# Reciprocal roots by Newton steps on VectorE, attention values with features on the partitions, low parts of weights on VectorE, and new tables of pulls

## The chip, the cores and the metric

The kernel runs on one core of a Trainium2 chip. A core has a matrix engine (TensorE, PE in the profile, its weight loads PEld), a vector engine (VectorE, DVE), a scalar engine (ScalarE, ACT), a general engine (GpSimd, POOL) and DMA queues (SP among others). Each engine works through its own queue in order, and semaphores hold an instruction until its inputs are there. The metric is the device time of one execution, in microseconds (us); before it is 652.63 us, the median of 3 runs (649.9 to 655.0).

## The reference

One layer of a streaming encoder over 512 tokens with 1024 features, cut to what is computed:

```
h = RMSNorm(x) * (1 + scale) + shift            # scale, shift, gate = adaLN(c)
p = h @ w_in                                    # one projection, split among the branches
y_a = RWKV7(p_a) * silu(g_a) @ w_a_out          # 8 heads of 64, decayed state, group norm
y_b = DSA(p_b) * silu(g_b) @ w_b_out            # 8 heads of 64, q and k RMS-normalised per head
m = sigmoid(p_ga) * y_a + sigmoid(p_gb) * y_b
x + gate * (m @ w_o)
```

The recurrence of RWKV7 is linear and is solved in chunks of 64 tokens. DSA scores the keys of each query with 8 small index heads, keeps the best (at most 128 here, within the chunks that are allowed), and takes a softmax over those:

```
idx_score = sum_h relu(iq_h @ ik) * iw_h;  sel = top_k(idx_score, 128)
p = softmax(q @ k_sel * 64**-0.5);  y = p @ v_sel
```

Everything is float32. The square roots are those of the RMS norm of x, of the norms of q and k, and of the group norm of the RWKV branch.

## The kernel before

**Precision.** A float32 operand of a large product is split in a high part that TensorE multiplies fast (type fp32r) and a low part, the rest. A projection is three products: high by high, low by high, high by low. Weights come by DMA from SP's queue (`wraw`), ScalarE copies the high part (`whi`, `whigh`), and a subtraction makes the low part (`wlo`, `wlow`, L247). Which engine subtracts is set by the block's place in the list of filler blocks: block 0 on VectorE, blocks 1 to 13 on GpSimd as soon as the high part is asked for, the later ones on VectorE two steps of the filler later (list `later`).

**Stages.** (1) Front, 0 to 64 us: x, its norm, adaLN, the transposes. (2) Index scores with the rates of decay, 64 to 135. (3) Preparation, 135 to 237: products, bonus and Gram matrices of the RWKV heads. (4) Solve, 237 to 311: triangular systems, column by column, on VectorE: a product (`pt`, L704) and a sum (`XT`, L706) for the even and the odd blocks. (5) Chain, 311 to 362: eight chunks in turn with a state `SV`. (6) Attention, 362 to 549: 32 jobs (4 pairs of heads, 4 blocks of 128 queries, 2 heads). (7) Merge and output, 549 to 648.

**What sets the order.** After the front the order is that of the code. A generator `main()` writes stages 2 to 6 piece by piece and yields after each piece two numbers: so many us of filler to draw into TensorE's queue (`pull`) and so many of side work to draw into VectorE's (`pull_dve`: top-k, group norm). The filler is the 24 projection blocks that the branches need later (`projections()`), about 10 us each; the side work of a finished block (copies on ScalarE, shifts on VectorE, roots) follows it through `later`. The tables `GT` and `DT` at the end of the function give the two numbers of the first 129 pieces; behind them, in the attention, defaults hold (1.3 us after each of two pieces of a job).

**A job of the attention.** `scores` makes two products into `ps_a`; one VectorE operation (L889) adds the mask and takes the minimum; ScalarE takes the exponential with its sum (`lg`, `sm`). One job later `flip` turns `lg` 128 columns at a time on TensorE, and ScalarE copies the result to `pT`. For each two jobs `values` multiplies `pT` (stationary, 128x128) by 64 columns of `vt`, so that tokens lie on the partitions; VectorE takes the reciprocal of the two sums (L913) and multiplies (L915, `yt`); `turn` transposes `yt` on TensorE into `ps_z`, and after four blocks one multiplication by the gate (L927) writes 128x512 of `yb`.

**Roots.** `qk_stats` (4 calls) and the group norm (2 calls) each take a square root on ScalarE, then a reciprocal on VectorE; `qk_stats` follows with one Newton step, and GpSimd scales `qn` by it (L833). ScalarE loads a table of functions (ACT_TABLE_LOAD) when it goes from an exponential to a root and back.

Of the kernel before, what the change touches and what calls it, by code (L numbers as in the profile page):

```python
# [37 lines left out]
def hybrid_block_kernel(ctx, tc, x, c, norm_w, w_ada, b_ada, w_in, mu, w0, w_up, a0, a_up, k_k, k_a,  # L38
# [67 lines left out]
    eps6 = cp.tile([128, 1], F32, name="eps6")  # L106
    V.memset(eps6, EPS)
    epsg = cp.tile([128, 1], F32, name="epsg")
    V.memset(epsg, GN_EPS)
# [18 lines left out]
    ss = cp.tile([128, NT], F32, name="ss")  # L128
    for i in range(NT):
        junk = T("LX6", [128, D], bufs=2, name="junk")  # L130
        act(junk, xt(i), AF.Square, accum_out=ss[:, i:i + 1])
    act(ss, ss, AF.Sqrt, scale=1.0 / D, bias=eps6)
    V.reciprocal(ss, ss)
    for i in range(NT):
        act(xt(i), xt(i), AF.Copy, scale=ss[:, i:i + 1])

# [735 lines left out]
    def attention():  # L872
# [45 lines left out]
        def turn():  # L918

            p, i, yt = st.pop("y")  # L920
            if i == 0:
                st["z"] = bank("z")
            tr(st["z"][:, i * 128:(i + 1) * 128], yt.rearrange("p s d -> p (s d)"), ident)
            if i == NT - 1:
                if p % 2 == 0:
                    ybt.append(T("kr", [128, 2, S], bufs=2, name="yb"))
                V.tensor_mul(ybt[p // 2][:, p % 2, :], st.pop("z"), sgb[p])  # L927
# [468 lines left out]
```

## Time and profile before

The profiled execution took 649.95 us, of which the span from its first to its last instruction is 648.2 us; the rest lies around it.

| stage, us | length | PE busy | DVE busy | ACT busy | POOL busy | granted clock |
|---|---|---|---|---|---|---|
| front 0-64 | 64 | 46.97 | 40.82 | 35.93 | 11.76 | 1.00 |
| index 64-135 | 71 | 59.66 | 47.37 | 44.27 | 15.26 | 0.92 |
| preparation 135-237 | 102 | 100.93 | 73.81 | 41.64 | 52.34 | 0.99 |
| solve 237-311 | 74 | 60.60 | 65.48 | 27.39 | 31.52 | 0.93 |
| chain 311-362 | 51 | 45.86 | 30.88 | 22.17 | 6.37 | 0.93 |
| attention 362-549 | 187 | 164.86 | 95.57 | 97.01 | 4.83 | 0.93 |
| merge, output 549-648 | 99 | 95.06 | 62.87 | 21.39 | 0.00 | 1.00 |

Busy us are read against the length of the stage: the engine with the largest share is the candidate for what bounds it, and the waits of the others say on whom they wait. The granted clock is that of TensorE, as a share of its full speed. An idle time in brackets names the instruction that ended it. Busy of TensorE counts a matmul until its modelled end.

### The profile page before, as it was taken

What the parts mean: (1) busy time and instruction counts of PE and PEld (TensorE: products, weight loads), DVE (VectorE), ACT (ScalarE), POOL (GpSimd) and SP (SyncE); (2) the same over time, 40 slices, a digit from 0 to 9 for tenths busy, and PEclk for the clock granted to TensorE, in tenths of its full rate; (3) what the DMA queues carried; (4) which work ended last, traced back from release to release, by engine and by line L of the source; (5) the groups of instructions that cost most, each with busy time, mean ns of one, the idle gap of its engine ahead of it and who ended that gap; (6) DMA issues with size and microseconds to landing.
All of it is one profiled execution on the core that took longest, in us unless ns stands there. A gap on an engine that the chain in (4) does not pass through costs nothing.

```text
span 648.2 us, 10436 instructions
## 1 busy us (share of the span) xinstructions
PE 573.9 (89%) x4051; PEld 475.2 (73%) x4051; DVE 416.8 (64%) x904; ACT 289.8 (45%) x521; POOL 122.1 (19%) x138
## 2 busy tenths in 40 slices
PE   1899888899999986997898799977987999999997
PEld 0677546567677966896776678876766888998997
DVE  4794537898769559996576664654554344888542
ACT  7743755652353333327433455555644445322210
POOL 7000202235264582352211000101000000000000
PEclk9999979989999997998799899968987999999999
DMA  9990312226546732145564121120212222656331
GB/s 300 320 332 10 98 32 66 66 47 166 139 122 167 170 101 73 46 130 147 179 231 148 29 70 52 48 65 19 75 39 65 66 66 81 179 176 205 115 122 66
DMA packets 80637, 75.00 MB, mean 116 GB/s; under 512 B 15737, under 2 KB 76226, under 8 KB 80588
## 3 DMA queue, kind: packets, MB, share of 16 engines
q1 hardware_dynamic: 74492, 59.86, 31.3%
q0 software_dynamic: 3776, 12.22, 6.2%
q10 hardware_dynamic: 2320, 2.26, 1.1%
q8 instruction: 32, 0.52, 0.3%
q14 instruction: 17, 0.14, 0.1%
HBM read 62.63 MB, written 11.55 MB: 114 GB/s over the span
## 4 chain that ended last, share of the span: by engine, by line
PE 58%; DVE 22%; ACT 13%; issue 3%; DMA 2%; POOL 1%; SPq 0%; POOLq 0%; ACTq 0%; DVEq 0%
PE ps_pj L46 32%; PE ps_yc L46 9%; PE ps_a L46 6%; DVE pt L704 5%; PE ps_o L46 3%; PE ps_z L46 3%; DVE XT L706 2%; ACT whi L87 2%; PE ps_a L49 2%; PE ps_yc L49 2%; DVE bias L90 2%; DVE wlo L247 2%; ACT qd L87 1%; DVE qd L90 1%; ACT L87 1%
## 5 line engine op out<-in xcount | busy, mean ns | idle before, releaser
L46 PE MATMUL ps_pj<-hh,whi 128*128 128x512 f32 (+1 forms) x304 | 126.5, 418 | 2.4 <-ACT hh L87 2.4
L46 PE MATMUL ps_pj<-hh,wlo 128*128 128x512 f32 (+1 forms) x304 | 127.2, 418 | 1.1 <-POOL wlo L247 1.1
L46 PE MATMUL ps_pj<-hl,whi 128*128 128x512 f32 (+1 forms) x304 | 126.3, 416 | 0.2 <-DVE hl L191 0.2
L247 POOL TENSOR_TENSOR wlo<-wraw,whi 128x1024 fp32r<-128x1024 f32 (+1 forms) x38 | 64.9, 1725 | 138.0 <-ACT whi L87 121.1
L87 ACT ACTIVATE whi<-wraw 128x1024 fp32r<-128x1024 f32 (+2 forms) x80 | 71.2, 918 | 26.7 <-DVE xr L1224 19.2
L46 PEld LDWEIGHTS ps_pj<-hh,whi 128*128 128x128 f32 (+1 forms) x304 | 59.5, 196 | 16.1 <-ACT hh L87 3.1
L46 PEld LDWEIGHTS ps_pj<-hh,wlo 128*128 128x128 f32 (+1 forms) x304 | 59.3, 195 | 16.3 <-issue 3.0
L46 PE MATMUL ps_pj<-whi,hh 128*128 128x256 f32 x192 | 58.8, 306 | 12.2 <-DVE sga L90 6.3
L46 PEld LDWEIGHTS ps_pj<-hl,whi 128*128 128x128 f32 (+1 forms) x304 | 59.5, 196 | 13.2 <-DVE hl L191 1.2
L247 DVE TENSOR_TENSOR wlo<-wraw,whi 128x1024 fp32r<-128x1024 f32 (+1 forms) x42 | 50.4, 1210 | 27.2 <-ACT whi L87 27.1
L46 PE MATMUL ps_pj<-wlo,hh 128*128 128x256 f32 x192 | 57.0, 297 | 0.4 <-POOL wlo L247 0.4
L46 PE MATMUL ps_pj<-whi,hl 128*128 128x256 f32 x192 | 56.9, 296 | 0.0
L46 PEld LDWEIGHTS ps_pj<-whi,hh 128*128 128x128 f32 x192 | 39.2, 204 | 14.1 <-DVE sga L90 7.0
L46 PEld LDWEIGHTS ps_pj<-wlo,hh 128*128 128x128 f32 x192 | 39.4, 205 | 0.7 <-POOL wlo L247 0.6
L46 PEld LDWEIGHTS ps_pj<-whi,hl 128*128 128x128 f32 x192 | 39.2, 204 | 0.0
L46 PE MATMUL ps_pj<-whi,mh 128*128 128x256 f32 x128 | 36.4, 285 | 0.0
L46 PE MATMUL ps_pj<-wlo,mh 128*128 128x256 f32 x128 | 36.0, 281 | 0.0
L46 PE MATMUL ps_pj<-whi,ml 128*128 128x256 f32 x128 | 36.0, 281 | 0.0
L87 ACT ACTIVATE lg<-lg,mx 128x128 f32<-128x128 f32 (+3 forms) x32 | 18.0, 562 | 38.7 <-DVE mx L889 27.2
L704 DVE TENSOR_TENSOR pt<-XT,PNO 128x2 f32<-128x2 f32 (+45 forms) x61 | 31.6, 557 | 0.1
L833 POOL TENSOR_TENSOR qn<-qn,s 128x256 f32<-128x256 f32 x16 | 11.1, 720 | 101.5 <-DVE s L90 79.1
L90 DVE SCALAR_TENSOR_TENSOR qd<-ps_a,P,qd 64x256 fp32r<-64x256 f32 x32 | 15.5, 483 | 20.1 <-ACT qd L87 20.1
(286 smaller groups left out, 1205.3 us busy)
## 6 DMA issues: line engine op xcount, KB each, us to landing
wraw<-in_w_in_dram SPq DMA_DIRECT2D x44, 512.0 KB
wa<-in_w_ada_dram SPq DMA_DIRECT2D x32, 256.0 KB
lxc<-dLX POOLq DMA_DIRECT2D x8, 768.0 KB, 5.3
wraw<-in_w_in_dram SPq DMA_DIRECT2D x18, 256.0 KB
dLX<-lx SPq DMA_DIRECT2D x8, 512.0 KB
wraw<-in_w_ada_dram SPq DMA_DIRECT2D x8, 512.0 KB
wraw<-in_w_o_dram SPq DMA_DIRECT2D x8, 512.0 KB
x<-in_x_dram SPq DMA_DIRECT2D x4, 512.0 KB
```

The costliest lines, as they stand in the source:

```text
L46: return nc.tensor.matmul(*a, **k)
L49: return nc.tensor.transpose(*a, **k)
L87: A.activation(o, i, func, **kw)
L90: V.scalar_tensor_tensor(o, a, s, b, op0=op0, op1=op1, **kw)
L247: eng.tensor_sub(l_, r_, f(h_))
L704: V.tensor_mul(pv[e], XT[e][:, a0:, j + 1:], PN[:, j, None, j + 1:].to_broadcast([128, m, n]))
L706: V.tensor_reduce(XT[e][:, (j + 2 - e) // 2:, j], pv[e], axis=AX.X, op=ALU.add)
L833: G.tensor_mul(qv, qv, bc(y[:, i, :]))
```

## The change

- A function `rsqrt` makes a reciprocal root of small tiles with 12 VectorE operations: an addition, a shift of the bits, a start value from integers, and three Newton steps of three operations. It takes the place of the square root on ScalarE and of the reciprocal in the norm of x (now in two pairs of token blocks), in `qk_stats` and in the group norm.
- `norm` divides the exponentials in place before they are turned: a reciprocal of a 128x1 tile and a multiplication of `lg` (128 to 512 columns) for each of the 32 jobs.
- `values` has 64 features of `vt` as the stationary tile and 128 columns of `pT` moving; the two heads of a job pair write the two halves of the partitions of one bank, banks `o` and `z` by turns. One multiplication by the gate (128x128) for each two jobs writes `yb`. `turn`, `yt` and the four large multiplications by the gate go.
- Low parts: all on VectorE, all through `later`. 22 subtractions of 128x1024 and 16 of 128x256 change their engine.
- The tables of pulls now cover all pieces (0 to 201). Added up, the drawn filler runs behind that of before by 2.5 us from piece 1 on, by 3 us or so through preparation and solve, is 1.8 us ahead from piece 105 (the end of the solve), 6.8 us ahead by piece 128 (the end of the chain), and 7 to 9.7 us ahead in the attention. The sum of the filler is the same.

```
+    def rsqrt(y, t_, u, eps, c):
+        V.tensor_scalar(u, u, eps, None, op0=ALU.add)
+        V.tensor_scalar(t_.bitcast(I32), u.bitcast(I32), 1, None, op0=ALU.logical_shift_right)
+        V.tensor_scalar(y.bitcast(I32), t_.bitcast(I32), -1.0, 1597463007.0, op0=ALU.mult, op1=ALU.add)
+        for k in (1.0, 1.0, c):
+            stt(t_, y, -0.5 * k, y, ALU.mult, ALU.mult)
+            V.tensor_mul(t_, t_, u)
+            stt(y, t_, 1.5 * k, y, ALU.add, ALU.mult)
...
             def low():
-                wlow(G if i < NPOOL else V, raw, hi, lo, 256, blocks[i][1])
+                wlow(V, raw, hi, lo, 256, blocks[i][1])
                 w_load()
-            if i < NPOOL:
-                low()
-            else:
-                later.append([2, low])
+            later.append([2, low])
...
     def qk_stats(g, j, s2, qn):
-        act(y, s2, AF.Sqrt, scale=1.0 / HD, bias=eps6)
-        V.reciprocal(y, y)
-        V.tensor_scalar(s2, s2, -0.5 / HD, -0.5 * EPS, op0=ALU.mult, op1=ALU.add)
-        V.tensor_mul(t_, y, y)
-        V.tensor_mul(t_, t_, s2)
-        stt(y, t_, 1.5, y, ALU.add, ALU.mult)
-        if j == 0:
-            V.tensor_scalar(y, y, -0.125, None, op0=ALU.mult)
+        rsqrt(y, t_, s2, EPS * HD, HD ** 0.5 if j else -1.0)
...
+        def norm(n):
+            p, i, s = jobs[n]
+            lg, sm = st[n], sums[p, i][:, s:s + 1]
+            V.reciprocal(sm, sm)
+            V.tensor_scalar(lg[:, :128 * (i + 1)], lg[:, :128 * (i + 1)], sm, None, op0=ALU.mult)
+
         def values(n):
-            ps = bank("o")
-            for s in range(2):
-                pT = st.pop(n + s)
-                for j in range(i + 1):
-                    mm(ps[:, 64 * s:64 * s + 64], pT[:, j * 128:(j + 1) * 128],
-                       vts[j // 2][:, j % 2, (2 * p + s) * 64:(2 * p + s + 1) * 64], start=(j == 0), stop=(j == i))
-            sm = sums.pop((p, i))
-            V.reciprocal(sm, sm)
-            yt = T("on", [128, 2, 64], bufs=2, name="yt")
-            V.tensor_mul(yt, ps[:, 0:128].rearrange("p (s d) -> p s d", d=64), bc(sm))
-            st["y"] = p, i, yt
+            pTs = [st.pop(n + s) for s in range(2)]
+            ps = bank("oz"[n // 2 % 2])
+            for j in range(i + 1):
+                for s in range(2):
+                    mm(ps[half(s), :128], vts[j // 2][:, j % 2, (2 * p + s) * 64:(2 * p + s + 1) * 64],
+                       pTs[s][:, j * 128:(j + 1) * 128], start=(j == 0), stop=(j == i))
+            ts_ = slice(i * 128, (i + 1) * 128)
+            V.tensor_mul(ybt[p // 2][:, p % 2, ts_], ps[:, :128], sgb[p][:, ts_])
...
+                if n:
+                    norm(n - 1)
                 scores(n)
                 yield gp(f"at1.{p}.{i}.{n % 2}")
             if n % 2 and n >= 3:
                 values(n - 3)
-            if n % 2 == 0 and n >= 4:
-                turn()
...
-        104: 2.404, 105: 2.512, 106: 2.635, 107: 0.78, 108: 2.528,
+        104: 2.404, 105: 5.754, 106: 2.635, 107: 0.78, 108: 2.748,
-        126: 1.751, 127: 4.016, 128: 0.054}
+        126: 1.969, 127: 6.028, 128: 0.347, 129: 0.82, 130: 1.08,
```

VectorE's queue in the solve before, from the sums behind the 105-column products on; `pt` and `XT` are the products and sums of the columns, and MATCH_REPLACE is a piece of the top-k.

```order
L706 TENSOR_REDUCE XT<-pt 128x7
L706 TENSOR_REDUCE XT<-pt 128x8
L516 MATCH_REPLACE bias_586<-m_2163,bias_586 128x512
L704 TENSOR_TENSOR pt<-XT,PNO 128x128 x2
L706 TENSOR_REDUCE XT<-pt 128x8 x2
L704 TENSOR_TENSOR pt<-XT,PNO 128x136
L704 TENSOR_TENSOR pt<-XT,PNO 128x153
L706 TENSOR_REDUCE XT<-pt 128x8
L706 TENSOR_REDUCE XT<-pt 128x9
```

The same place in the changed kernel; `wlo` is the low part of a weight, L1118 a sum of squares for the norm of q or k.

```order
L709 TENSOR_REDUCE XT<-pt 128x7
L709 TENSOR_REDUCE XT<-pt 128x8
L254 TENSOR_TENSOR wlo<-wraw,whi 128x1024
L519 MATCH_REPLACE bias_605<-m_2202,bias_605 128x512
L707 TENSOR_TENSOR pt<-XT,PNO 128x128 x2
L709 TENSOR_REDUCE XT<-pt 128x8 x2
L1118 TENSOR_REDUCE s_2178<-sq 128x4
L707 TENSOR_TENSOR pt<-XT,PNO 128x136
L707 TENSOR_TENSOR pt<-XT,PNO 128x153
L709 TENSOR_REDUCE XT<-pt 128x8
L709 TENSOR_REDUCE XT<-pt 128x9
L254 TENSOR_TENSOR wlo<-wraw,whi 128x1024
```

Two subtractions of 128x1024 now stand among the columns, where there was none; before, GpSimd's queue held them.

VectorE's queue in the attention before, from the first 512-key job to the first job of the next pair of heads; `lg,mx` is the mask step of a job, `ya` a piece of the other branch's output.

```order
L889 ISA lg,mx<-ps_a,bias_586 128x512
L889 ISA mx 128x1
L90 SCALAR_TENSOR_TENSOR ya<-ps_a,P_559,sga 128x256
L1031 TENSOR_TENSOR ya__3765<-ya,ya__3764 128x256
L90 SCALAR_TENSOR_TENSOR ya<-ps_a,P_559,sga 128x256
L1031 TENSOR_TENSOR ya__3765<-ya,ya__3764 128x256
L889 ISA lg,mx<-ps_a,bias_586 128x512
L889 ISA mx 128x1
L913 RECIPROCAL sm<-sm 128x2
L915 TENSOR_TENSOR yt<-ps_o,sm 128x128
L889 ISA lg,mx<-ps_a,bias_583 128x128
L889 ISA mx 128x1
```

The same jobs in the changed kernel, from the division of the first 512-key job on.

```order
L902 RECIPROCAL sm<-sm 128x1
L903 TENSOR_SCALAR lg<-lg,sm 128x512
L885 ISA lg,mx<-ps_a,bias_605 128x512
L885 ISA mx 128x1
L91 SCALAR_TENSOR_TENSOR ya<-ps_a,P_578,sga 128x256
L1020 TENSOR_TENSOR ya__3835<-ya,ya__3834 128x256
L91 SCALAR_TENSOR_TENSOR ya<-ps_a,P_578,sga 128x256
L1020 TENSOR_TENSOR ya__3835<-ya,ya__3834 128x256
L917 TENSOR_TENSOR yb<-ps_o,sgb 128x128
L902 RECIPROCAL sm<-sm 128x1
L903 TENSOR_SCALAR lg<-lg,sm 128x512
L885 ISA lg,mx<-ps_a,bias_602 128x128
```

The division of job n-1 (L902, L903) now stands ahead of the mask step of job n, and behind the pieces of `ya`, so that it is the exponential's sum for which VectorE may wait there; the step that writes `yb` reads TensorE's result with the gate, where `yt` was multiplied by the reciprocal.

TensorE's queue before, at the first values of a 512-key block; `ps_pj` is filler.

```order
L46 MATMUL ps_pj<-whi,hh 128x256
L46 MATMUL ps_pj<-wlo,hh 128x256
L46 MATMUL ps_pj<-whi,hl 128x256
L46 MATMUL ps_o<-vt,pT 128x64 x8
L49 MATMUL ps_yc<-ident,lg 128x128
```

And in the changed kernel.

```order
L47 MATMUL ps_pj<-whi,hh 128x256
L47 MATMUL ps_pj<-wlo,hh 128x256
L47 MATMUL ps_pj<-whi,hl 128x256
L47 MATMUL ps_z<-pT,vt 64x128 x8
L50 MATMUL ps_yc<-ident,lg 128x128
```

The eight products of the place stay eight; moving and stationary operand have changed sides, the output has 64 partitions and 128 columns, and the row for `ps_z<-ident,yt`, one for each two jobs before, is in TensorE's queue no more. ScalarE's queue holds one ACT_TABLE_LOAD in place of 15.

## Rows read from the trace of the kernel before

**Rows 1.** The page, part 1: busy us of each engine, its share of the span, and the count of its instructions.

```profile
PE 573.9 (89%) x4051; PEld 475.2 (73%) x4051; DVE 416.8 (64%) x904; ACT 289.8 (45%) x521; POOL 122.1 (19%) x138
```

**Rows 2.** The windows view, one row for each of five stages: the window, its length, busy us (and instructions) of PE, PEld, DVE, ACT and POOL, then the granted TensorE clock, the DMA share and GB/s. The stages are the index scores (64 to 135), the preparation (135 to 237), the solve (237 to 311), the chain (311 to 362) and the attention (362 to 549).

```profile
64.00:135.00 71.00, 59.66 (x243) 40.24 (x242) 47.37 (x83) 44.27 (x76) 15.26 (x7) 0.92 0.23 63
135.00:237.00 102.00, 100.93 (x585) 77.13 (x585) 73.81 (x172) 41.64 (x74) 52.34 (x64) 0.99 0.53 136
237.00:311.00 74.00, 60.60 (x540) 55.13 (x541) 65.48 (x165) 27.39 (x44) 31.52 (x20) 0.93 0.36 102
311.00:362.00 51.00, 45.86 (x891) 36.12 (x884) 30.88 (x69) 22.17 (x49) 6.37 (x12) 0.93 0.47 168
362.00:549.00 187.00, 164.86 (x916) 141.77 (x916) 95.57 (x241) 97.01 (x205) 4.83 (x8) 0.93 0.19 57
```

**Rows 3.** The waits of TensorE (PE), added up by what ended them: us in total, how often, the longest.

```profile
PE ps_pj L46 <- DVE sga L90: 6.3, 2, 3.5
PE ps_o L46 <- ACT pT L87: 6.0, 4, 2.6
PE ps_a L46 <- ACT rl L87: 4.8, 5, 2.1
PE ps_yc L46 <- ACT Et L87: 4.8, 3, 2.3
PE ps_a L49 <- POOL qn L833: 4.3, 4, 3.4
```

**Rows 4.** The timeline of VectorE (DVE) among the index scores: start, duration, line and operation, output <- inputs, and in brackets the idle time ahead of it and what ended it.

```profile
98.42 0.48 DVE L90 SCALAR_TENSOR_TENSOR bias<-rl,iw,bias 128x256 f32<-128x256 f32 x1
99.24 2.46 DVE L90 SCALAR_TENSOR_TENSOR bias<-rl,iw,bias 128x256 f32<-128x256 f32 x1 [0.35 <-ACT rl L87]
...
119.47 2.22 DVE L504 TENSOR_SCALAR bias<-rl,iw 128x512 f32<-128x512 f32 x1 [0.42 <-ACT rl L87]
```

**Rows 5.** The timeline of GpSimd (POOL) in the same stretch, the first of its four operations there.

```profile
99.01 2.41 POOL L247 TENSOR_TENSOR wlo<-wraw,whi 128x1024 fp32r<-128x1024 f32 x1 [17.93 <-ACT whi L87]
```

**Rows 6.** The timeline of VectorE in the solve: products and sums of the columns; x2 is two operations in one row.

```profile
238.78 2.33 DVE L704 TENSOR_TENSOR pt<-XT,PNO 128x2 f32<-128x2 f32 x2
...
255.70 3.93 DVE L704 TENSOR_TENSOR pt<-XT,PNO 128x128 f32<-128x128 f32 x2
...
259.93 0.52 DVE L704 TENSOR_TENSOR pt<-XT,PNO 128x136 f32<-128x136 f32 x2
...
274.32 4.54 DVE L704 TENSOR_TENSOR pt<-XT,PNO 128x338 f32<-128x338 f32 x2
...
282.77 2.35 DVE L704 TENSOR_TENSOR pt<-XT,PNO 128x392 f32<-128x392 f32 x2
```

**Rows 7.** The timeline of GpSimd in the solve, one of its six rows.

```profile
273.23 7.88 POOL L247 TENSOR_TENSOR wlo<-wraw,whi 128x1024 fp32r<-128x1024 f32 x3
```

**Rows 8.** The groups of instructions by line and form, VectorE: count, busy us, mean ns of one, idle time ahead.

```profile
L247 DVE TENSOR_TENSOR wlo<-wraw,whi 128x1024 fp32r<-128x1024 f32 x40 | 48.4, 1222 | 27.2 <-ACT whi L87 27.1
...
L915 DVE TENSOR_TENSOR yt<-ps_o,sm 128x128 f32<-128x128 f32 x16 | 4.7, 292 | 16.7 <-PE ps_o L46 16.1
...
L889 DVE CUSTOM_DVE_ANT_0 lg<-ps_a,bias 128x512 f32<-128x512 f32 x8 | 5.5, 690 | 7.7 <-PE ps_a L46 7.6
...
L913 DVE RECIPROCAL sm<-sm 128x2 f32<-128x2 f32 x16 | 2.5, 159 | 0.0
...
L171 DVE TENSOR_SCALAR acc<-wa,silu_c 128x512 f32<-128x512 f32 x4 | 1.9, 482 | 0.0
...
L827 DVE TENSOR_TENSOR s<-s,s 128x16 f32<-128x16 f32 x4 | 0.7, 176 | 0.1
```

**Rows 9.** The same view for ScalarE (ACT).

```profile
L87 ACT ACT_TABLE_LOAD x15 | 19.2, 1283 | 2.4 <-issue 2.1
...
L87 ACT ACTIVATE lg<-lg,mx 128x512 f32<-128x512 f32 x8 | 5.8, 723 | 13.0 <-DVE mx L889 7.1 <-DVE sm L913 5.9
```

**Rows 10.** The timeline of ScalarE in the attention: the first of its eight loads of a function table there with the square root behind it, and the last load.

```profile
361.49 1.28 ACT L87 ACT_TABLE_LOAD   x1
362.78 0.31 ACT L87 ACTIVATE st<-st,epsg 128x16 f32<-128x16 f32 x1
...
456.20 1.28 ACT L87 ACT_TABLE_LOAD   x1
```

**Rows 11.** The groups by line and form, TensorE, of the attention alone; two records stand for each of these products.

```profile
L46 PE MATMUL ps_o<-vt,pT 128*128 128x64 f32 x160 | 20.7, 273 | 6.0 <-ACT pT L87 6.0
...
L49 PE MATMUL ps_z<-ident,yt 128*128 128x128 f32 x16 | 4.6, 289 | 0.0
```

**Rows 12.** The timeline of TensorE in the attention: six products of the values (12 records) and the turning of exponentials behind them.

```profile
397.62 1.45 PE L46 MATMUL ps_o<-vt,pT 128*128 128x64 f32 x12
398.91 0.61 PE L49 MATMUL ps_yc<-ident,lg 128*128 128x128 f32 x4
```

**Rows 13.** The timeline of TensorE in the chain: 32 records of products with a 64-wide stationary tile and 64 moving columns, in the two halves of the output partitions by turns, between filler products.

```profile
319.10 0.40 PE L46 MATMUL ps_pj<-hh,whi 128*128 128x512 f32 x1
319.33 0.40 PE L46 MATMUL ps_pj<-hh,wlo 128*128 128x512 f32 x1
319.66 1.15 PE L46 MATMUL ps_yc<-SV,lxc 128*64 128x64 f32 x32
320.74 0.50 PE L46 MATMUL ps_pj<-hl,whi 128*128 128x512 f32 x1
```

More of the change, by code (lines that the diff above doesn't have):

```diff
@@ L8 @@
 F32R = mybir.dt.float32r
+I32 = mybir.dt.int32
 AF = mybir.ActivationFunctionType
@@ L105, in hybrid_block_kernel @@
     V.memset(ones, 1.0)
[L106 to L109, printed above, removed]
     sel = cp.tile([128, 2], F32, name="sel")
@@ L125, in hybrid_block_kernel @@
     V.tensor_mul(sc_, sc_, cT)
[L128 to L135, printed above, removed]
+    def rsqrt(y, t_, u, eps, c):
[6 more added lines that the diff above has]
+            stt(y, t_, 1.5 * k, y, ALU.add, ALU.mult)
+    for p in range(2):
+        ss = cp.tile([128, 6], F32, name=f"ss{p}")
+        for i in range(2):
+            junk = T("LX6", [128, D], bufs=2, name="junk")
+            act(junk, xt(2 * p + i), AF.Square, accum_out=ss[:, i:i + 1])
+        rsqrt(ss[:, 2:4], ss[:, 4:6], ss[:, 0:2], EPS * D, D ** 0.5)
+        for i in range(2):
+            act(xt(2 * p + i), xt(2 * p + i), AF.Copy, scale=ss[:, 2 + i:3 + i])
     sh = cp.tile([128, KT], F32, name="sh")
@@ L345, in hybrid_block_kernel @@
     raws, his_los = {}, {}
-    NPOOL = PR["order"].index("s")
     GATE0 = len(PR["order"]) - 1
@@ L901, in flip @@
             st[n] = pT
+        def norm(n):
[3 more added lines that the diff above has]
+            V.tensor_scalar(lg[:, :128 * (i + 1)], lg[:, :128 * (i + 1)], sm, None, op0=ALU.mult)
         def values(n):
             p, i, _ = jobs[n]
-            ps = bank("o")
-            for s in range(2):
-                pT = st.pop(n + s)
-                for j in range(i + 1):
-                    mm(ps[:, 64 * s:64 * s + 64], pT[:, j * 128:(j + 1) * 128],
-                       vts[j // 2][:, j % 2, (2 * p + s) * 64:(2 * p + s + 1) * 64], start=(j == 0), stop=(j == i))
-            sm = sums.pop((p, i))
-            V.reciprocal(sm, sm)
-            yt = T("on", [128, 2, 64], bufs=2, name="yt")
-            V.tensor_mul(yt, ps[:, 0:128].rearrange("p (s d) -> p s d", d=64), bc(sm))
-            st["y"] = p, i, yt
[L918 to L927, printed above, removed]
+            pTs = [st.pop(n + s) for s in range(2)]
+            if n % 8 == 0 and p % 2 == 0:
+                ybt.append(T("kr", [128, 2, S], bufs=2, name="yb"))
+            ps = bank("oz"[n // 2 % 2])
[5 more added lines that the diff above has]
+            V.tensor_mul(ybt[p // 2][:, p % 2, ts_], ps[:, :128], sgb[p][:, ts_])
         N = len(jobs)
-        for n in range(N + 3):
+        for n in range(N + 2):
             p = n // 8
@@ L939, in attention @@
                 values(n - 3)
-            if n % 2 == 0 and n >= 4:
-                turn()
             if 0 <= n - 1 < N:
+                if n == N:
+                    norm(n - 1)
                 flip(n - 1)
@@ L997, in group_norm @@
                 V.tensor_reduce(st2[:, ci, :], sq, axis=AX.X, op=ALU.add)
-            act(st2[:, cs], st2[:, cs], AF.Sqrt, scale=1.0 / HD, bias=epsg)
-            V.reciprocal(st2[:, cs], st2[:, cs])
+            rsqrt(st1[:, cs], T("s4", [128, NT, 4], bufs=2, name="gt"), st2[:, cs], GN_EPS * HD, HD ** 0.5)
             yield 0.6
             for ci in range(4 * g, 4 * g + 4):
-                V.tensor_mul(Y[:, ci - 4 * g], Y[:, ci - 4 * g], bc(st2[:, ci, :]))
+                V.tensor_mul(Y[:, ci - 4 * g], Y[:, ci - 4 * g], bc(st1[:, ci, :]))
                 V.tensor_mul(Y[:, ci - 4 * g], Y[:, ci - 4 * g], gnw_bc)
@@ L1330, in main @@
         done.add("main")
-    GT = {0: 3.808, 1: 2.495, 2: 1.186, 3: 0.87, 4: 0.87, 5: 1.026, 6: 0.317, 7: 0.48, 8: 0.896, 9: 0.545, 10:
[13 rows of a table removed]
-    DT = {0: 0, 1: 0, 2: 0.3, 3: 0, 4: 0, 5: 0.0, 6: 0.3, 7: 0, 8: 0.3, 9: 0, 10: 0, 11: 0.3, 12: 0, 13: 0, 14:
[10 rows of a table removed]
+    GT = {0: 3.808, 1: 0, 2: 1.186, 3: 1.896, 4: 0.87, 5: 0, 6: 0.317, 7: 0.48, 8: 0.896, 9: 0.545, 10: 0.597, 11:
[19 rows of a table added]
+    DT = {0: 0, 1: 0, 2: 0.3, 3: 0, 4: 0, 5: 0, 6: 0.3, 7: 0, 8: 0.3, 9: 0, 10: 0, 11: 0.3, 12: 0, 13: 0, 14: 0, 15:
[17 rows of a table added]
     n = 0
```

2 lines of the change are left out of this document (removed), and 59 rows, old and new, of tables (DT, GT).

## The prediction

> **What bounds the kernel now.** I read the page first: TensorE is busy for 573.9 of 648.2 us, VectorE for 416.8 [rows 1]. That is an average, so the windows came next [rows 2]. In the preparation TensorE has 100.93 of 102 us; it alone bounds. In the solve VectorE has the larger share (65.48 of 74, TensorE 60.60): the columns run there one behind the other, and TensorE fills. The index scores and the attention have no full engine: in the attention TensorE idles 22 of 187 us, in the index scores 11 of 71, in the chain 5 of 51, and in all of these and the solve the granted clock is 0.92 or 0.93 against 0.99 in the preparation. The waits of TensorE say on whom [rows 3]: roots and their users on GpSimd (`qn`, 4.3 us), ScalarE's copies (`pT` 6.0, `rl` 4.8, `Et` 4.8), and `sga` (6.3), which stands in VectorE's queue among the columns. Then I asked what holds VectorE. One operation on `bias` takes 0.48 us, the same form at 99.24 takes 2.46, and it ends when GpSimd's subtraction that began at 99.01 ends (101.42) [rows 4, 5]. The columns show the same: 3.93 us for a pair of 128 columns, 0.52 for a pair of 136 [rows 6], 4.54 for a pair of 338 while GpSimd subtracts from 273.23 on [rows 7].
>
> **The change part by part.** The sum is made against the profiled execution, 649.95 us; the median of the runs is 652.63, 0.4% above.
>
> *Low parts.* A subtraction of 128x1024 takes VectorE 1.22 us [rows 8]. Each stalled operation costs it about as much as GpSimd needs, some 2.4 less the head start, so every such stall that goes pays for the work that comes.
> Index scores: three stalls of about 2.0 and one of 1.7 (2.22 less some 0.5 for an operation of 512 columns [rows 4, 8]) go, 7.7 us; four to six subtractions come, 4.9 to 7.3. VectorE gains 0.4 to 2.8, but `rl`'s 4.8 us of waits are mostly the echo of these stalls. With one table load less ahead of `Et` (1.28 [rows 9]) I take **-4.5**; bounds -9 (nearly all of `rl` and `Et`) and +1.
> Preparation: eight subtractions of 1.22 and sixteen of a quarter of the width (about 0.42, estimated between 0.29 for 128 columns and 1.22 for 1024) come, 16 us. VectorE goes from 73.8 to 90 of 102 [rows 2]. TensorE's filler is the cover; if a block's low part comes late, TensorE waits for one or two of 1.22. I take **+1.5**, bounds 0 and +4.
> Solve: the stalls sum to 12 us (2.05 in the first pair, 3.4, 3.6, 1.3 in the last, the rest between [rows 6]); six subtractions (7.3 us) come between the columns, and one `rsqrt` is longer by about 1 us on VectorE. That is -3.7 on the engine that bounds; the two `sga` waits (6.3) shrink with it. I take **-5**, bounds -9 and 0.
>
> *Roots.* `rsqrt` is 12 operations of about 0.176 [rows 8], 2.1 us. Before, VectorE waited for a table load and the root, 1.28 + 0.31 [rows 10], and then did five or six small operations, about 1: 2.5 us. That path is equal within 0.4. What goes is ScalarE's time: 14 loads of 1.283, 18 us [rows 9], of which the attention has eight, 10.3 [rows 10]. ScalarE is half busy there (97.01 of 187), so less than half is on a path: TensorE's waits for `pT` and `qn` (10.3 together [rows 3]) are where it shows. I take **-3.5** in the attention, bounds -8 and 0. The norm of x in two pairs lets the first flips start earlier, but its two Newton runs add 2 us to a front that waits for DMA and adaLN: 0, bounds -1 and +1.
> The Trainium skill (ScalarE: Activation LUTs, What ACT_TABLE_LOAD costs) puts a switch of tables at about 2.66 us, 1283 ns of load and some 1380 of a drain. The trace agrees with the load and shows no drain: the load of 361.49 ends at 362.77 and the root starts at 362.78 [rows 10]. By the page 14 switches would free 37 us and the attention's term would be near -7, by the row 18 and -3.5.
>
> *Values.* Six products (12 records) take 1.29 us from the first to what follows [rows 12], 0.107 a record; 160 records [rows 11] are 17.2 us at full clock. A product with 64 columns stationary, in halves by turns, 32 records of 64 moving columns, takes 1.08 us from start to next, 0.034 a record [rows 13]; with 128 moving columns I double it: 160 x 0.068 = 10.8. This holds the turn into and out of the halves, about 0.1 each (0.33 in place of 0.23 between two starts [rows 13]). 16 transposes, some 0.11 each, go as well: 1.8. Together -8.2; **-8** in the attention, bounds -11 (the busy time of rows 11, tails and all) and 0 (the halves don't run side by side: 80 products of 128 columns cost what they cost before).
>
> *Division in place.* It adds a reciprocal of about 0.16 and a multiplication of 0.22 to 0.48 (0.482 for 512 columns [rows 8]) for each of 32 jobs, 16.2 us, and 16 multiplications of 0.29; it removes 2.5 and 4.7 [rows 8] and the four gates of 128x512, some 0.69 each as the mask step of that size: net +10.6 on VectorE, which has 95.57 of 187. The cost is its place: between exponential and flip, on the path of a job, 0.4 to 0.65, and ahead of the next mask step in VectorE's queue. What covers it is filler, 2.6 us a job. I take **+4**, bounds +1 and +10.
>
> *Pulls.* The filler is constant. 6.8 us more of it by the end of the chain moves from the attention: **-6.5** there, and in the chain **+2.5**, since it has 5 us of idle TensorE [rows 2] for part of it; bounds 0 and +5.
>
> The sum: -4.5 + 1.5 - 5 + 2.5 - 14 (= -3.5 - 8 + 4 - 6.5) = **-19.5**, so **630 us**. TensorE's idle time then is some 15 us less, and the rest is work that goes.
>
> **The rivals.**
> *More comes back: 615.* Stages at 0.92 or 0.93 with levels of 1.2 and 2.4 GHz spent about 14% of their 383 us at the lower level, where each us does half; that is about 27 us. If the vanished waits keep the clock up as in the preparation (0.99), half of it returns: 630 - 14 = 616, and more of `pT` and `rl` brings 615. For it: each stage that waits has the low clock. Against: most of TensorE's waits in the attention are for the jobs' own chain, which gets longer.
> *Only moved: 648.* The stalls of VectorE were hidden anyway, and the subtractions take what they leave: index 0, preparation +4, solve -1, chain +4; attention -9 (values -5, loads 0, division +3, pulls -7). That is -2, 648. For it: VectorE's sum rises by some 30 us, and the stalls and the subtractions differ by little. Against: 12 us of stalls lie on the columns, one behind the other.
> *The halves do not overlap: 638.* Then the values cost as before, 630 + 8. The Trainium skill (TensorEngine Tiling (Array Packing), Key Properties) says that a change of tiling mode drains TensorE. The trace shows 0.1 us a change, and 32 changes are 3 us, within the 10.8 above. Against this rival: rows 13 at 0.034 a record against 0.107.
> *VectorE's turn around a job closes: 664.* Mask step of job n now stands behind the division of job n-1, which waits for that job's exponential. Mask 0.69, exponential 0.72 [rows 8, 9], reciprocal 0.16, multiplication 0.48: 2.05 us for a 512-column job, in which VectorE and ScalarE do nothing else if they stand still for each other. VectorE has 2.5 us of other work a job (95.57 / 32 less the mask), together 4.55; TensorE has 5.15 a job now, about 4.7 after the gains. So it just holds. If 1 us of ScalarE's other copies (it is busy for 97.01 of 187 [rows 2]) stands ahead of each exponential, it is 5.6, and lateness of 1.2 us a job, 38 us in place of the 4, gives 664. It decides from 0.9 us a job on. Against: a job holds side work that fills VectorE's wait, and jobs of 128 and 256 columns have a shorter turn.
>
> **How the numbers follow.** Forecast (617 to 643) 0.53, more comes back 0.15, no overlap of halves 0.08, only moved 0.14, closed turn 0.10. All terms at their low bounds give 609, at their high ones about 662; 609 to 652 leaves out the closed turn and the ends, under 2 in 10; the likeliest case alone is 617 to 643. A measurement of this kernel can tell about 1% from no change: faster 0.76 (the first three), same 0.14, slower 0.10.
>
> **What would show it.** The mean of `pt` pairs at 128 columns is 0.5 and no stall ends with a GpSimd operation; the solve is about 5 us shorter. One ACT_TABLE_LOAD. The records of the values stand 0.07 apart, 16 groups. TensorE's waits on `qn` and `pT` fall below 10.3, waits on `lg` grow by less than 4. In the preparation TensorE stays above 98 of 100. The forecast is wrong if the preparation gets longer by more than 4, if TensorE's waits on `lg` exceed 10 (closed turn), or if the filler moved ahead lengthens the chain by the whole 6.8.

## The result, and the profile after

The changed kernel takes 628.72 us, the median of 4 runs (626.8 to 632.27), against 651.26 (649.23 to 655.0) before. The ratio is 0.9654 with a 95% interval of 0.9589 to 0.9719: 3.5% faster. 630 us were predicted.

The profiled execution took 632.27 us, the slowest of the four, so its stages add up to 3.5 us more than the median. The page, part 1, answers to [rows 1]:

```profile
PE 564.6 (90%) x4035; PEld 460.0 (73%) x4035; DVE 443.8 (70%) x1055; ACT 268.6 (43%) x500; POOL 62.3 (10%) x100
```

VectorE is busy 27 us more and GpSimd 60 less. The windows of five stages follow (length, busy us and instructions of PE, PEld, DVE, ACT, POOL, then granted clock, DMA share, GB/s). They answer to [rows 2], but are cut at events that both kernels have, as the table of stages below: index scores, preparation, columns of the solve, chain, attention.

```profile
83.56:134.88 51.32, 51.32 (x209) 34.94 (x208) 38.19 (x73) 33.61 (x61) 0.93 (x1) 0.87 0.21 57
134.88:230.82 95.94, 95.94 (x572) 75.41 (x572) 83.27 (x196) 37.95 (x69) 28.49 (x42) 1.00 0.55 153
230.82:280.12 49.30, 43.85 (x329) 41.32 (x328) 47.35 (x155) 14.09 (x26) 5.83 (x7) 1.00 0.30 94
304.10:351.95 47.85, 40.56 (x767) 32.27 (x767) 26.59 (x62) 16.54 (x40) 6.46 (x12) 0.89 0.42 139
351.95:522.83 170.88, 148.05 (x859) 119.59 (x860) 108.79 (x317) 82.21 (x188) 6.65 (x8) 0.96 0.19 56
```

In the kernel before, the index scores at the same cuts were:

```profile
83.82:140.04 56.22, 49.34 (x202) 33.53 (x202) 41.06 (x69) 34.36 (x62) 11.40 (x6) 0.92 0.16 44
```

The index scores and the preparation have no idle time of TensorE left in this execution. In the index scores 6.9 us of it went, but the stage got only 4.9 shorter, since the granted clock is 0.87 and not 0.92. The attention still has 22.8 us of it (170.88 - 148.05), as many as before (22.1), though they stand elsewhere. The waits of TensorE, which answer to [rows 3]:

```profile
PE ps_yc L50 <- DVE lg L903: 12.6, 7, 4.6
...
PE ps_pj L47 <- ACT sq L88: 4.5, 3, 2.4
PE ps_pj L47 <- DVE sga L91: 4.0, 2, 3.5
...
PE ps_a L50 <- POOL qn L829: 2.6, 2, 2.4
...
PE ps_yc L47 <- ACT Et L88: 2.0, 1, 2.0
...
PE ps_pj L47 <- DVE wlo L254: 1.5, 2, 1.3
```

`rl` and `pT` are gone, `Et` and `qn` have shrunk, and a new first row has come: the division of the exponentials (`lg`, L903), 12.6 us in 7 waits. The longest, 4.6 us, stands ahead of the attention's first turning; the run without any division (e4 below) still waits 4.0 us there, so some 8.6 of the 12.6 belong to the division. The groups of VectorE and the one load of ScalarE (count, busy us, mean ns of one, idle ahead) answer to [rows 4, 6, 8, 9]:

```profile
L91 DVE SCALAR_TENSOR_TENSOR bias<-rl,iw,bias 128x256 f32<-128x256 f32 x7 | 3.4, 482 | 4.0 <-ACT rl L88 3.9
...
L902 DVE RECIPROCAL sm<-sm 128x1 f32<-128x1 f32 x32 | 5.0, 156 | 3.1 <-ACT lg L88 3.0
...
L903 DVE TENSOR_SCALAR lg<-lg,sm 128x512 f32<-128x512 f32 x8 | 3.9, 486 | 0.3
...
L707 DVE TENSOR_TENSOR pt<-XT,PNO 128x338 f32<-128x338 f32 x2 | 0.9, 494 | 0.0
```

```profile
L88 ACT ACT_TABLE_LOAD x1 | 1.3, 1283 | 2.1 <-issue 2.1
```

The index scores' form takes 482 ns on the mean, a product of 338 columns 494, where a pair took 4.54 us; the stalls are gone.

Where the time went is read from stage lengths, each worked out as the difference of two starts in the timeline: first copy `rl`, first Gram product, product of `PNO`, last `pt`, first copy `SV`, last copy `Y`, last exponential, first `mh`, last `oo`. The names of the experiments are explained below.

| kernel | front | index | preparation | columns | solve's end | chain | attention | to merge | merge |
|---|---|---|---|---|---|---|---|---|---|
| before | 83.8 | 56.2 | 96.9 | 54.4 | 23.6 | 46.2 | 180.1 | 17.9 | 85.4 |
| after | 83.6 | 51.3 | 95.9 | 49.3 | 24.0 | 47.9 | 170.9 | 18.5 | 85.4 |
| e1 lows gpsimd | 82.8 | 57.1 | 100.9 | 54.6 | 23.4 | 46.5 | 170.9 | 18.5 | 85.3 |
| e2 roots scalar | 84.2 | 49.6 | 95.2 | 48.1 | 24.0 | 46.6 | 167.9 | 18.5 | 85.9 |
| e3 tokens first | 83.6 | 51.1 | 95.8 | 49.3 | 24.0 | 47.9 | 161.2 | 20.4 | 85.9 |
| e4 no division | 83.5 | 51.1 | 95.5 | 49.3 | 23.9 | 47.9 | 156.8 | 18.3 | 85.4 |
| e5 old tables | 83.4 | 52.2 | 95.5 | 51.0 | 25.6 | 46.1 | 193.0 | 18.6 | 85.3 |
| e6 division early | 83.4 | 49.6 | 95.6 | 49.3 | 24.1 | 47.7 | 161.8 | 18.4 | 85.9 |
| e7 before lows | 85.5 | 52.4 | 95.3 | 50.1 | 26.0 | 46.6 | 181.0 | 17.9 | 85.9 |
| e9 roots and values back | 83.4 | 49.6 | 95.2 | 48.1 | 24.0 | 46.1 | 160.6 | 20.4 | 85.3 |
| e10 attention defaults | 83.6 | 49.6 | 96.2 | 49.3 | 23.4 | 45.7 | 188.7 | 23.1 | 85.8 |
| e11 roots back division early | 83.0 | 51.2 | 95.2 | 48.1 | 24.9 | 46.0 | 160.1 | 18.4 | 85.3 |
| e12 before new tables | 86.5 | 57.5 | 97.7 | 55.7 | 24.7 | 47.6 | 160.5 | 20.4 | 85.3 |
| e13 attention filler default | 83.5 | 51.2 | 95.5 | 49.3 | 23.4 | 46.0 | 194.9 | 18.8 | 85.4 |

Stages with the same code differ between profiled executions: the index scores take 51.3 us in the changed kernel and 49.6 in e6 and e10, the chain 47.9 and in e10 45.7. A difference of up to 2 us in one stage thus shows nothing by itself.

By stages the sum came out near the forecast: index -4.9 (forecast -4.5), preparation -1.0 (+1.5), solve -4.7 with its end (-5), chain +1.6 (+2.5), attention -9.2 (-14). The preparation missed the forecast's sign and the attention fell 4.8 short. Whether the terms inside came out, the experiments had to tell.

### The profile page after: what moved, and what is told of

Same layout as the page of the kernel before. It is cut to its first block, busy times and chain, and to the rows that moved or that the text cites. A ratio compares the mean times of both kernels' runs of the same rounds, so it can differ in the third digit from the quotient of the medians.

```text
span 630.6 us, 10459 instructions
## 1 busy us (share of the span) xinstructions
PE 564.6 (90%) x4035; PEld 460.0 (73%) x4035; DVE 443.8 (70%) x1055; ACT 268.6 (43%) x500; POOL 62.3 (10%) x100
## 4 chain that ended last, share of the span: by engine, by line
PE 62%; DVE 22%; ACT 8%; issue 3%; DMA 2%; SPq 1%; ACTq 0%; DVEq 0%
PE ps_pj L47 36%; PE ps_yc L47 10%; PE ps_a L47 8%; DVE wlo L254 3%; PE ps_z L47 3%; PE ps_a L50 2%; PE ps_yc L50 2%; DVE qd L91 2%; DVE pt L707 2%; ACT whi L88 1%; ACT qd L88 1%; DVE XT L709 1%; PE ps_o L47 1%; DMA x<-in_x_dram 1%; DVE lg L885 1%
## 5 line engine op out<-in xcount | busy, mean ns | idle before, releaser
L254 DVE TENSOR_TENSOR wlo<-wraw,whi 128x1024 fp32r<-128x1024 f32 (+2 forms) x80 | 83.7, 1064 | 22.5 <-ACT whi L88 22.5
L88 ACT ACTIVATE whi<-wraw 128x1024 fp32r<-128x1024 f32 (+2 forms) x80 | 71.4, 920 | 25.6 <-DVE xr L1213 19.2
L47 PE MATMUL ps_pj<-whi,hh 128*128 128x256 f32 x192 | 56.3, 293 | 7.2 <-DVE sga L91 4.0
L47 PE MATMUL ps_pj<-wlo,hh 128*128 128x256 f32 x192 | 54.9, 286 | 1.5 <-DVE wlo L254 1.5
L47 PE MATMUL ps_pj<-whi,hl 128*128 128x256 f32 x192 | 54.7, 285 | 0.0
L88 ACT ACTIVATE lg<-lg,mx 128x128 f32<-128x128 f32 (+3 forms) x32 | 18.0, 563 | 48.1 <-DVE mx L885 47.9
L47 PEld LDWEIGHTS ps_pj<-wlo,hh 128*128 128x128 f32 x192 | 37.0, 192 | 2.0 <-DVE wlo L254 1.9
L47 PEld LDWEIGHTS ps_pj<-whi,hl 128*128 128x128 f32 x192 | 36.9, 192 | 0.0
L50 PE MATMUL ps_yc<-ident,lg 128*128 128x128 f32 x80 | 15.3, 289 | 14.2 <-DVE lg L903 12.6
L517 DVE MAX8 m<-bias 128x8 f32<-128x256 f32 (+2 forms) x48 | 26.7, 557 | 0.9
L829 POOL TENSOR_TENSOR qn<-qn,s 128x256 f32<-128x256 f32 x16 | 15.4, 989 | 118.3 <-DVE s L91 100.6
L519 DVE MATCH_REPLACE8 bias<-m,bias 128x256 f32<-128x256 f32 (+2 forms) x48 | 26.0, 542 | 0.0
```

The costliest lines, as they stand in the source:

```text
L47: return nc.tensor.matmul(*a, **k)
L50: return nc.tensor.transpose(*a, **k)
L88: A.activation(o, i, func, **kw)
L254: eng.tensor_sub(l_, r_, f(h_))
L517: V.max(out=m8, in_=acc)
L519: V.match_replace(out=acc, in_to_replace=m8, in_values=acc, imm_value=MARK)
```

## The experiments

Ratios are to the kernel before, in runs on the same chip; us are medians. Three chips were used: one for e1 to e4, one for e5, e6, e9 and e11, one for e7, e10, e12 and e13. Across chips only ratios are compared. A difference of two ratios is turned into us with 652; with the two intervals taken as independent it carries some 4 to 6 us either way.

**Low parts.** Two runs: the changed kernel with its low parts on GpSimd again (e1), and the kernel before with the low parts on VectorE alone (e7).

```
-                wlow(V, raw, hi, lo, 256, blocks[i][1])
+                wlow(G if i < NPOOL else V, raw, hi, lo, 256, blocks[i][1])
...
-            later.append([2, low])
+            if i < NPOOL:
+                low()
+            else:
+                later.append([2, low])
```

> The changed kernel with the low parts of blocks 1 to 13 back on GpSimd, at once. If GpSimd's subtractions held VectorE and this was worth what the prediction booked (index scores about -3, solve -5, preparation +1.5): some 635 us, the stage of the index scores 3 longer, the columns of the solve (first product to last) 5 longer, preparation 1 shorter. Rival, stalls hidden under other waits: 628 to 631, with the stalls back in the trace.

> The kernel before with the low parts on VectorE and nothing else. If GpSimd's hold on VectorE is worth the same under the old tables: 634 to 637, with stalls gone from the index scores and the solve. By the prediction's terms for the low parts alone (-3, +1.5, -5): 644. Rival, without the new tables the subtractions on VectorE make TensorE wait: 650 or more.

e1: 645.33 us, 0.9873 [0.9808, 0.9938], some 14 us slower than the changed kernel. The index scores are 5.7 longer, the columns 5.3, and the preparation 5.0, where 1 in the other direction was expected. The stalls of VectorE are back: the two forms that took 482 and 494 ns on the mean in the changed kernel take 763 and 1212.

```profile
L91 DVE SCALAR_TENSOR_TENSOR bias<-rl,iw,bias 128x256 f32<-128x256 f32 x7 | 5.3, 763 | 3.9 <-ACT rl L88 3.8
...
L711 DVE TENSOR_TENSOR pt<-XT,PNO 128x338 f32<-128x338 f32 x2 | 2.4, 1212 | 0.0
```

TensorE waits for GpSimd's slower subtraction once near the preparation's end (2.69 us) and once in the solve (2.81):

```profile
PE ps_pj L47 <- POOL wlo L254: 5.5, 2, 2.8
```

The windows of that wait and of the stretch behind it show the rest of the preparation's 5.0:

```profile
230.80:233.68 2.88, 0.20 (x1) 0.00 (x0) 1.44 (x9) 0.00 (x0) 2.69 (x6) 0.87 0.07 11
233.68:239.50 5.82, 5.82 (x13) 4.16 (x14) 0.44 (x2) 0.69 (x1) 5.82 (x8) 0.50 0.31 90
```

Behind the wait TensorE runs 5.8 us at its lower level, 1.2 GHz (granted clock 0.50). Its products start 0.43 us apart there and 0.23 ahead of the wait, so some 2.7 us more are lost.

e7: 645.97 us, 0.9904 [0.9875, 0.9933], 6.2 us faster than before, near the 6.7 of the prediction's own terms, and the stalls are gone (483 and 493 ns for the same two forms). So the mechanism holds. The low parts are worth 6 us under the old tables and more under the new: 14 by e1, 19 by e9 against e12 below (with the norm of x in its new form).

**Roots.** The changed kernel with the square roots of the q, k and group norms on ScalarE again (e2); the norm of x keeps its Newton steps.

```
-        rsqrt(y, t_, s2, EPS * HD, HD ** 0.5 if j else -1.0)
+        act(y, s2, AF.Sqrt, scale=1.0 / HD, bias=eps6)
+        V.reciprocal(y, y)
...
-            rsqrt(st1[:, cs], T("s4", [128, NT, 4], bufs=2, name="gt"), st2[:, cs], GN_EPS * HD, HD ** 0.5)
+            act(st2[:, cs], st2[:, cs], AF.Sqrt, scale=1.0 / HD, bias=epsg)
+            V.reciprocal(st2[:, cs], st2[:, cs])
```

> The changed kernel with the roots back as square roots on ScalarE (x norm in its two pairs, q and k norms, group norm). The prediction booked -3.5 in the attention and 1.3 in the index scores: 633 to 634. If each switch of tables costs 2.66 us and half of that is on a path: 645. Rival, Newton's 12 operations on VectorE are as long as load and root together: 627 to 630, and TensorE's wait of 4.6 us ahead of the first flip gets no longer.

625.55 us, 0.9572 [0.9524, 0.962]: not slower without the Newton steps, and 3 us shorter in the attention. The pair e6 and e11 below, on one chip, makes it sure. The group norm, two of the six calls, shows a part of why. VectorE's timeline of the changed kernel, from the last sum to the first use, the 12 operations between (first and last shown):

```profile
353.16 0.42 DVE L987 TENSOR_REDUCE st<-sqy 128x4 f32<-128x256 f32 x1 [0.54 <-ACT sqy L88]
353.62 0.17 DVE L127 TENSOR_SCALAR st<-st 128x16 f32<-128x16 f32 x1
...
355.92 0.17 DVE L91 SCALAR_TENSOR_TENSOR st<-gt,st 128x16 f32<-128x16 f32 x1
356.12 0.42 DVE L991 TENSOR_TENSOR Y<-Y,st 128x256 f32<-128x256 f32 x1
```

And with the root on ScalarE:

```profile
348.94 0.42 DVE L998 TENSOR_REDUCE st<-sqy 128x4 f32<-128x256 f32 x1 [0.54 <-ACT sqy L88]
350.56 0.25 DVE L1000 RECIPROCAL st<-st 128x16 f32<-128x16 f32 x1 [1.20 <-ACT st L88]
350.85 0.42 DVE L1003 TENSOR_TENSOR Y<-Y,st 128x256 f32<-128x256 f32 x1
```

From the start of the sum to the first use it takes 2.96 us with Newton and 1.91 with the root. The 12 operations start 0.21 us apart, 2.5 us; the table's load ran while VectorE still summed, so that VectorE waited 1.20 us and not 1.6. How the rest of the gain is spread over the other calls was not followed.

**Values and division.** The changed kernel with values, division and transposes of before (e3), and without any division (e4; its values are not normalised).

```
-                if n:
-                    norm(n - 1)
...
             if n % 2 and n >= 3:
                 values(n - 3)
+            if n % 2 == 0 and n >= 4:
+                turn()
```

> The changed kernel with the values, the division and the transposes of before. By the prediction's terms (values -8, division +4): 633. By the trace after (7.5 us less of TensorE for the values and transposes, but 12.6 us of waits on divided exponentials): 626 to 630, waits on lg back to some 3 us. If the division were hidden: 636.

> The changed kernel without the division of the exponentials: no reciprocal of the sums and no multiplication, so the values are not normalised. If the division in VectorE's queue is what TensorE waits for: the 12.6 us of waits on lg fall below 5 and the time to 619 to 623. By the prediction's +4: 625. Rival, TensorE waits for ScalarE's copies or the side work instead: 627 or more.

e3: 623.57 us, 0.9541 [0.9489, 0.9593]; e4: 617.35 us, 0.9445 [0.9394, 0.9495]. The new form of the values with its division is slower than the old. Without its division it is 6.3 us faster than the old form (e4 against e3), near the prediction's -8. The division costs 13.6 us (the changed kernel against e4), where +4 was booked with 10 as the bound. In e4 TensorE's waits on divided exponentials are gone; one wait for an exponential itself is left:

```profile
PE ps_yc L50 <- ACT lg L88: 4.0, 1, 4.0
```

The attention is 14.1 us shorter in e4 (170.88 and 156.78), with the same instructions of TensorE: 8.9 of it are idle time, 5.2 busy time at a granted clock of 0.99 in place of 0.96. The timelines of ScalarE and VectorE in the changed kernel show what one of the waits is made of:

```profile
375.95 0.19 ACT L88 ACTIVATION_READ_ACCUMULATOR lg<-lg,mx 128x1 f32 x1
```

```profile
377.88 1.22 DVE L254 TENSOR_TENSOR wlo<-wraw,whi 128x1024 fp32r<-128x1024 f32 x1 [2.48 <-ACT whi L88]
379.02 0.42 DVE L991 TENSOR_TENSOR Y<-Y,st 128x256 f32<-128x256 f32 x1
379.47 0.42 DVE L992 TENSOR_TENSOR Y<-Y,gnw_bc 128x256 f32<-128x256 f32 x1
379.81 0.42 DVE L994 TENSOR_TENSOR bv<-Vt,bon 128x256 f32<-128x256 f32 x1
380.26 0.42 DVE L995 TENSOR_TENSOR Y<-Y,bv 128x256 f32<-128x256 f32 x1
380.61 0.15 DVE L902 RECIPROCAL sm<-sm 128x1 f32<-128x1 f32 x1
380.80 0.42 DVE L903 TENSOR_SCALAR lg<-lg,sm 128x384 f32<-128x384 f32 x1
```

The exponential's sum was there at 376.14, and the reciprocal starts at 380.61. Ahead of it in VectorE's queue stands a low part whose own input comes only at 377.88, so that VectorE is idle for 1.7 us with the division ready behind it; then come 2.7 us of the low part and the group norm. TensorE has done its values and waits for the turning:

```profile
379.22 0.66 PE L47 MATMUL ps_z<-pT,vt 128*64 128x128 f32 x8
381.36 0.52 PE L50 MATMUL ps_yc<-ident,lg 128*128 128x128 f32 x3 [1.48 <-DVE lg L903]
```

**The division's place.** The division right behind the first filler piece of its own job (e6), and the same with roots on ScalarE (e11).

```
-                if n:
-                    norm(n - 1)
                 scores(n)
                 yield gp(f"at1.{p}.{i}.{n % 2}")
+                norm(n)
```

> The changed kernel with the division of a job issued behind its first filler piece, ahead of the side work of the second, and not one job later. If TensorE waits because the division stands in VectorE's queue behind side work: the waits on lg fall from 12.6 to 6 or less and the time to 620 to 624. Rival, VectorE then waits for the exponential with its whole queue behind it: 629 or more, and VectorE's idle time ahead of the reciprocal grows from 3 to over 15 us.

> The changed kernel with roots on ScalarE and the early division, values with features first as in the change. If both loosen the same queue and the values keep their 4 to 7 us on TensorE: 616 to 620, the fastest so far that computes the reference. Rival, the early division only moves VectorE's wait: 625 or more.

e6: 623.17 us, 0.9585 [0.9558, 0.9613]; the attention is 9.1 us shorter in the profiled executions. e11: 617.12 us, 0.9492 [0.9468, 0.9517], the fastest here that computes the reference: 6 us ahead of e6, on the same chip, by the roots alone. In its attention VectorE is busy for 103.09 us and not 109.27. TensorE's wait for the division in e6, and VectorE's reciprocal with the idle time ahead of it:

```profile
PE ps_yc L50 <- DVE lg L903: 3.4, 2, 3.0
```

```profile
L902 DVE RECIPROCAL sm<-sm 128x1 f32<-128x1 f32 x32 | 5.1, 160 | 11.1 <-ACT lg L88 11.1
```

VectorE now stands still for 11.1 us ahead of reciprocals, against 3.1 in the changed kernel, and the time falls all the same: its wait for the exponential is the cheaper one here. The place is not the whole of the division's cost: e6 gives back some 5 of the 13.6 us, and e4 stays 9 us ahead of it by the ratios. What makes up that rest was not followed.

**Both back.** Low parts and tables alone (e9: e2 and e3 together; the norm of x keeps its new form).

> The changed kernel with both of the edits back that the last runs showed to cost time: roots on ScalarE, values with tokens first and the old division. What stays are low parts and tables. If the two gains add up (3 and 5): 620 to 621. Rival, they overlap, since both shorten VectorE's queue ahead of the same flips: 623 to 625.

618.24 us, 0.951 [0.9488, 0.9532]: the two gains add up within the noise (5 and 7 us by the ratios, 9 together). Two of the change's four parts thus cost some 9 us together.

**Tables.** The changed kernel with the old tables (e5), with the defaults from piece 129 on (e10), with the defaults for the filler alone there (e13), and the kernel before with the new tables alone (e12).

```
+    GT = {k: v for k, v in GT.items() if k < 129}
+    DT = {k: v for k, v in DT.items() if k < 129}     # e10; e13 has the first line alone
```

> The changed kernel with the tables of pulls of before (pieces 0 to 128, defaults behind). By the prediction the tables move 6.5 us out of the attention and 2.5 into the chain: 633. By the run with tokens first, whose attention was 19 us shorter than that of before although values and division were those of before: the tables are worth more than 10 us, 640 to 648, most of it in the attention. Rival, the tables only follow the other edits: within 3 us of 629.

> The changed kernel with the tables cut at piece 128, so that the attention draws by the defaults as before. The filler drawn ahead of the attention is the same in all kernels (it stops at the label that waits for the chain), so the 30 us between old and new tables must come from where in the attention it is drawn: 645 to 652, the attention some 20 us longer, TensorE's waits on divided exponentials near the 29 us of the run with old tables. Rival, the pieces ahead of 129 carry it: 629 to 635.

> The changed kernel with only the filler's table cut at piece 128; the side work on VectorE stays as in the new table. If the placing of filler carries the tables' gain: 645 to 650, close to the run with both cut. Rival, the side work's table carries it (division no longer behind side work): 629 to 634.

> The kernel before with the new tables and nothing else. The run with low parts and tables alone took 618.2, and low parts back on GpSimd cost 16.6 in the changed kernel: if the two are independent, 635. Rival, the tables only help with low parts on VectorE: 645 to 650, no change against before.

e5: 658.62 us, 1.0146 [1.0112, 1.018]. With the old tables the change is 1.5% slower than the kernel before. e10: 653.78, 1.0019 [0.9986, 1.0053]; e13: 654.34, 1.0032 [0.9998, 1.0067]. So some 24 of the 32 us between old and new tables hang on how the filler is drawn in the attention, and with the filler drawn by default VectorE's side table adds nothing. TensorE's wait for the division in e13:

```profile
PE ps_yc L50 <- DVE lg L903: 32.1, 16, 3.9
```

e12: 639.23 us, 0.9805 [0.9742, 0.9868]. Alone the tables bring 12.7 us, and in the attention 19.6. The attention's windows before and in e12, with the same instructions of the kernel before:

```profile
361.11:541.16 180.05, 157.91 (x872) 135.62 (x871) 92.62 (x235) 93.91 (x200) 4.83 (x8) 0.92 0.18 54
```

```profile
369.61:530.09 160.48, 149.36 (x871) 129.34 (x872) 91.75 (x237) 93.30 (x200) 6.85 (x8) 0.97 0.21 60
```

TensorE idles 22.1 us before and 11.1 in e12, and its busy time falls from 157.91 to 149.36. Outside the attention e12 is 11 us longer than before; with low parts on VectorE (e9) all of these but the one ahead of the merge are shorter again. Low parts alone (6.2) and tables alone (12.7) make 19, together 32. Why the new tables lengthen the early stages when GpSimd has the low parts was not tried further; TensorE's waits for GpSimd's low parts are 1.5 us before, 2.6 in e12 and 5.5 in e1.

## Why the prediction was right, and where its steps were wrong

The time and the direction were right, and most stages came near; of the terms, one was right, one roughly, and three failed, with errors of both signs that cancel. One of the prediction's own signs of being wrong came true: TensorE's waits on `lg` are 12.6 us, above 10 (8.6 without the one that e4 has too).

- *Low parts, -6.7*: right in mechanism and in size under the old tables (6.2). The rival "only moved" falls with e7. That they are worth 14 us in the changed kernel was not foreseen: the preparation was booked at +1.5 for work that VectorE takes over, and the slower engine's lateness (the two waits of e1, 5.5 us, and some 2.7 us at the lower clock behind one of them) was not booked on the other side. A reading was a little off: the stalled operation of [rows 4] ends at 101.70, 0.28 us behind the subtraction and not with it.
- *Values, -8*: the mechanism was right, the size somewhat large. Eight records, from start to next, with the step ahead of them, in e6 and in e12:

```profile
374.90 0.39 PE L47 MATMUL ps_pj<-hl,whi 128*128 128x512 f32 x1
375.22 0.66 PE L47 MATMUL ps_z<-pT,vt 128*64 128x128 f32 x8
375.81 0.55 PE L50 MATMUL ps_yc<-ident,lg 128*128 128x128 f32 x3
```

```profile
393.20 0.40 PE L46 MATMUL ps_pj<-hl,whi 128*128 128x512 f32 x1
393.44 1.00 PE L46 MATMUL ps_o<-vt,pT 128*128 128x64 f32 x8
394.28 0.50 PE L49 MATMUL ps_yc<-ident,lg 128*128 128x128 f32 x3
```

The eight take 0.59 us in place of 0.84, but the product ahead of them holds until 0.32 us after its start and not 0.24, so a group of eight saves 0.17 and the dropped transpose 0.11. Groups of 4, 8, 12 and 16 records take 0.37, 0.59, 0.81 and 1.02 us, where they took 0.39, 0.84, 1.29 and 1.73. Over the four pairs of heads that is 11.2 us in place of 17.0; with 1.4 for the sixteen holds ahead and -1.8 for the transposes the term comes to -6.2; e4 against e3, which drops the old division as well, gave -6.3. The prediction counted the step into the halves as held within its 10.8; it comes on top. The rival "halves do not overlap" falls.
- *Division, +4*: wrong step: "What covers it is filler, 2.6 us a job." What has to be covered is not the division's 0.4 to 0.65 us alone, but also what stands ahead of it in VectorE's queue, the waits of that work included. That accounts for the part that e6 gives back; the other 9 us stay open. The mechanism named in the rival "closed turn" (VectorE waits for the exponential) was not the one either: the reciprocal waited 3.1 us in all, and making it wait more (e6) gained time. That rival's price does not follow from its terms either: 5.6 against 4.7 us is 0.9 a job, 29 us and not 38.
- *Roots, -3.5 and -1.3*: wrong sign, about +6 by e11 against e6. "That path is equal within 0.4" took load and root as one wait; the load overlaps the sum ahead of it, and Newton's operations start 0.21 us apart, not 0.176. In the group norm that is about 1 us a call; the rest of the +6 stays open. That ScalarE gave back 18 us was true (one load is left), and no gain from it shows.
- *Pulls, -6.5 and +2.5*: wrong. "6.8 us more of it by the end of the chain moves from the attention" added up the tables. What the tables ask for is not what is drawn: the next block waits for the label of the chain's end, and the filler runs dry: up to the end of the chain the trace has 916 records of filler products before and 912 after. The windows of the filler's products alone (`ps_pj`), three stretches of the chain after:

```profile
322.00:332.00 10.00, 2.64 (x9) 1.54 (x9) 0.00 (x0) 0.60 (x1) 1.00 0.52 168
332.00:342.00 10.00, 0.00 (x0) 0.00 (x0) 0.00 (x0) 0.00 (x0) 0.66 0.32 112
342.00:351.95 9.95, 0.00 (x0) 0.00 (x0) 0.00 (x0) 0.00 (x0) 1.00 0.26 94
```

The section on the change ahead of the prediction has the same fault, where it says that the filler runs ahead by 6.8 us: the tables do, the filler doesn't. What the tables bring comes for the most part from where the attention draws its constant filler (24 of 32 us). The chain's +1.6 is thus no sign that the term was right: the chain has less filler than before, not more (9.2 us of TensorE's busy time against 14.8), and with the same code up to its end e10 takes 45.7 us there, less than the 46.2 before.

The forecast of 630 against 628.72 is thus no proof of its terms. Division and roots together were off by some 20 us, tables and low parts together (-32 in e9, where -10.7 was booked) by 21 the other way. That they cancel is luck. The ends of the range were added up wrongly by some 1.5 us (609 and 662, where the terms give about 607 and 664); nothing rests on that.

## What to carry to other kernels

A small operation on the path can cost what stands ahead of it in its engine's queue, and the waits of that work, on top of its own duration; try it where its input comes ready, even if the engine then waits. Work moved off an engine that is half idle (ScalarE's table loads here) bought nothing that shows, and where it replaced a wait that ran beside other work, it cost time. When a schedule table and kernel edits change together, time the table alone and the edits alone: here the edits without the table were slower than before.
